# An encoder trunk in three-product float32: the DMA turn split into two steps, and another place for the seven-product units of w_down

## The chip, the cores and the metric

One core of a Trainium2 chip runs the whole program in one launch. The metric is the device time in microseconds (us), lower is better. Engine names are those of the profile: PE (TensorE matmul; its weight loads are PEld), DVE (VectorE), ACT (ScalarE), POOL (GpSimd), SP (SyncE, which here only issues DMAs). A small q behind a name (ACTq, SPq) is that engine's sequencer, which issues DMAs.

## The reference

Two layers over 256 tokens of width 2048, all float32. What matters here is the feed-forward half of each layer; the mixer ahead of it ends in a residual sum.

```python
def swiglu(h, w_gate_up, w_down):
    gate, up = jnp.split(h @ w_gate_up, 2, axis=-1)
    return (jax.nn.silu(gate) * up) @ w_down

for l in range(DEPTH):                       # DEPTH = 2, D_MODEL = 2048, D_FF = 5632
    ...                                      # token mixer, memory attention
    x = x + jnp.concatenate([tok_out, mem_out], axis=-1) @ w_out[l]
    x = x + swiglu(rms_norm(x, g_ffn[l]), w_gate_up[l], w_down[l])
```

## The kernel before

Every float32 product is made of three matmuls in a narrower type: a weight block is cast by ACT to `whi` (line 266), DVE subtracts to get the rest `wlo` (line 267), the activations are split in the same way, and `matmul3` (lines 199 to 201) issues hi x hi, hi x (the activation's rest) and (the weight's rest) x hi. All matmuls of the feed-forward half are 128x128 by 128x512.

The feed-forward half works in three chunks of the hidden width: gate/up columns 0 to 3, 4 to 7, and 8 to 10 (each 512 wide), and after each chunk the matching rows of `w_down`. A gate/up column and each half of `w_down` (called a and b here, 1024 output columns each) is one `Pair`: two blocks of 512 columns, both 128-token tiles. A `Pair` walks a list `order` of units; a unit is two 128-row blocks of the inner dimension against the two column blocks. Most units are computed with eight products (24 matmuls, method `eight`). Some, the quick ones, need seven (21 matmuls, method `seven`): DVE makes sums of weight blocks in place and in a tile `T` (lines 359 to 362), which is then cast and subtracted like a weight block. Sums of activations come from `activation_sums`. The quick units of a `Pair` also gather in four banks of their own (`m`); after the last of them, `inner` empties these into `e` tiles (lines 409 to 413) and, for `w_down`, adds them to the residual `x` (line 417). The other four banks (`acc`) are emptied by `outer` (line 425).

Between gate/up and `w_down` the gated activations must be transposed. `turned` does this with the DMA: ACT copies the tile into two planes of 16 bits (line 211), ACT's queue issues a transposing DMA (line 212), and ACT copies the result back into float32 order (line 215). ACT executes its instructions in order, so whatever stands behind line 215 waits for the landing. `turn_a` then splits the result for the matmuls. `add_residual` turns `x` in the same way at the end of a sub-layer.

The order of work is set by three things. The program counts steps: each half of a unit is one `tick`, and `later(n, f)` runs `f` n ticks on, so a turn is written between the units of the next `Pair`. The framework's scheduler then orders each engine's instructions: by the written order as a priority, but an instruction that is ready earlier by its own estimate may go ahead. And the buffers bound how far an engine runs ahead: three tiles for `whi` and for `wlo`, four for `raw` (the loaded weights), four `acc` and four `m` banks, 26 tiles for everything that `big` hands out.

The places of the quick units in `w_down` before: in half a third and fifth, in half b first and third (first and second chunk of a layer).

Of the kernel before, what the change touches and what calls it, by code (L numbers as in the profile page):

```python
# [12 lines left out]
U16 = mybir.dt.uint16  # L13
# [4 lines left out]
P = 128  # L18
# [36 lines left out]
def encoder(ctx: ExitStack, tc: tile.TileContext, x, mem, g_mix, g_ffn, w_in_a, g_v_a, w_spatial, b_spatial,  # L55
            w_in_b, g_q_b, g_k_b, g_mem, w_mem_kv, g_mq, g_mk, w_out, w_gate_up, w_down, rope_c, rope_s, out):
    nc = tc.nc
# [14 lines left out]
    def nm(s):  # L72
        uid[0] += 1
        return f"{s}_{uid[0]}"

    def big(dt=F32, shape=None):
        return room["p"].tile(shape or [P, NB], dt, tag="a", name=nm("a"))

    def small(n, long=False):
        return sp.tile([P, n], F32, tag=f"{'r' if long else 's'}{n}", name=nm(f"s{n}"), bufs=8 if long else 6)  # L80
# [4 lines left out]
    def v4(a):  # L85
        return a.rearrange("p (c n) -> p c n", n=P)
# [10 lines left out]
    def later(delay, fn):  # L97
        queue.append((clock[0] + delay, len(queue), fn))
# [22 lines left out]
    X = [[xp.tile([P, NB], F32, name=f"x_{t}_{j}") for j in range(4)] for t in range(NT)]  # L121
# [16 lines left out]
    def gslice(kind, l):  # L138
        return gcol[kind][:, 16 * l:16 * l + 16]
# [40 lines left out]
    def rsqrt_mean(ss, n, width, r=None):  # L180

        m = small(n)
        nc.gpsimd.tensor_scalar(m, ss, 1.0 / width, EPS, ALU.mult, ALU.add)
        if r is None:
            r = small(n, long=True)
        nc.gpsimd.tensor_tensor(r, m, mhalf[:, :n], ALU.pow)
        return r

    def split(src, shape):

        hi = big(F32R, shape)
        lo = big(F32R, shape)
        nc.scalar.copy(hi, src)
        nc.vector.tensor_tensor(lo, src, hi.bitcast(F32), ALU.subtract)  # L194
        return hi, lo
# [8 lines left out]
        for c in range(4):  # L204
            nc.tensor.transpose(dst[:, c * P:(c + 1) * P], src[:, c * P:(c + 1) * P], ident)  # L205

    def turned(src):

        a, b = big(F32, [P, 4, P]), big(F32, [P, 4, P])
        planes = a.bitcast(U16).rearrange("p c n -> p (c n)")  # L210
        nc.scalar.copy(planes.rearrange("p (h n) -> p h n", h=2), src.bitcast(U16).rearrange("p (n h) -> p h n", h=2))
        nc.scalar.dma_start_transpose(b.bitcast(U16).rearrange("p c n -> p (c n)").rearrange("p (c n) -> p c n", n=P),
                                      planes)
        whole = b.bitcast(U16).rearrange("p c n -> p (c n)").rearrange("p (h n) -> p n h", h=2)
        nc.scalar.copy(planes.rearrange("p (n h) -> p n h", h=2), whole)  # L215
        return a

    def square_sum(src, out):
        for i in range(2):
# [2 lines left out]
    def norm_piece(src, t, j, g, parts, keep):  # L222

        tp = misc()
        transpose4(src, tp)
        gained(tp, t, j, g, parts, keep)
        return tp
# [4 lines left out]
    def gained(tp, t, j, g, parts, keep):  # L232

        hi = keep(F32R, [P, 4, P])
        lo = keep(F32R, [P, 4, P])
        for c in range(4):
            gc = g[:, 4 * j + c:4 * j + c + 1]
            nc.scalar.activation(hi[:, c, :], v4(tp)[:, c, :], AF.Copy, scale=gc)
            nc.vector.scalar_tensor_tensor(lo[:, c, :], v4(tp)[:, c, :], gc, hi[:, c, :].bitcast(F32), ALU.mult,
                                           ALU.subtract)  # L240
            parts.put(4 * j + c, t, hi[:, c, :], lo[:, c, :])
        parts.whole[j, t] = hi, lo

    class Norm:
# [8 lines left out]
        def finish(self, out=(None, None)):  # L253
            self.r = []
            for t in range(NT):
                tot = small(1)
                nc.vector.tensor_reduce(tot, self.ss[t], AX.X, ALU.add)
                self.r.append(rsqrt_mean(tot, 1, D, out[t]))
# [53 lines left out]
    def activation_sums(a0, a1):  # L312

        q = big(F32, [P, 4, P])
        nc.vector.tensor_tensor(q[:, 0], a1[:, 0], a1[:, 1], ALU.subtract)
        nc.vector.tensor_tensor(q[:, 2], a1[:, 0], a0[:, 0], ALU.subtract)
        nc.vector.tensor_tensor(q[:, 1], a0[:, 0], q[:, 0], ALU.subtract)
        nc.vector.tensor_tensor(q[:, 3], a0[:, 1], q[:, 1], ALU.subtract)
        hi, lo = split(q, [P, 4, P])
        return [(hi[:, i, :], lo[:, i, :]) for i in range(4)]  # L320
# [277 lines left out]
    def add_residual(acc, j, norm, g, parts, dma):  # L598

        def turn(t):  # L600
            if dma:
                gained(turned(X[t][j]).rearrange("p c n -> p (c n)"), t, j, g, parts, kept)
            else:
                norm_piece(X[t][j], t, j, g, parts, kept)
            norm.add(X[t][j], t, j)
            if j == 3 and t == NT - 1:
                norm.finish()

        for t in range(NT):
            if acc:  # L610
                nc.vector.tensor_tensor(X[t][j], acc[t], X[t][j], ALU.add)
            later(1 + t, lambda t=t: turn(t))

    def residual_turns(j, norm, g, parts):
        add_residual(None, j, norm, g, parts, j < 2)
# [4 lines left out]
    for l in range(DEPTH):  # L620
# [105 lines left out]
        else:  # L726
# [12 lines left out]
            for c in range(3):  # L739
                acc = linear(hT, w, c * NB)  # L740
                attend(head_norm(acc, norm.r, ghead["q"], True), (5, 6, 10, 13), lambda: own["k"], lambda: own["v"],
                       lambda h, c=c: (4 * c + h) // 3, 4 * c, cat)
# [32 lines left out]
        for chunk in (range(0, 4), range(4, 8), range(8, 11)):  # L775
            aT, aS, half = Parts(), {}, {}
            quick = [2 * f + 1 for f in chunk[:2 if chunk[-1] < 10 else l]]

            def turn_a(a, t, f, aT=aT, aS=aS, half=half, quick=quick):
                whole = turned(a)  # L780
                i = 2 * f + 1
                if i in quick:
                    half[i, t] = big(F32, [P, 2, P])
                    nc.scalar.copy(half[i, t], whole[:, 2:4])
                    if t == NT - 1:
                        aS[i] = activation_sums(half[i, 0], half[i, 1])
                hi, lo = split(whole, [P, 4, P])
                for i in range(4):
                    aT.put(4 * f + i, t, hi[:, i, :], lo[:, i, :])

            pairs = {}
            for f in chunk:
                order, some = ((3, 4, 5, 0, 6, 1, 7, 2), 2) if f == 0 else ((0, 3, 1, 4, 2, 5, 6, 7), 3)
                pairs[f] = Pair(hF, sums, w_gate_up[l], f * NB, DFF + f * NB, order, fast[:some])
            for f, g in pairs.items():
                g.run(pairs.get(f + 1))
                for t in range(NT):
                    a = kp.tile([P, NB], F32, tag="sg", name=nm("sg"), bufs=2)
                    nc.scalar.activation(a, g.out[t][0], AF.Silu, scale=norm.r[t])
                    nc.vector.scalar_tensor_tensor(a, g.out[t][1], norm.r[t], a, ALU.mult, ALU.mult)  # L800
                    later(3 + t if f == chunk[-1] else 12 + t, lambda a=a, t=t, f=f: turn_a(a, t, f))
            last = chunk[-1] == 10
            every = [2 * f + c for f in chunk for c in range(2)]
            slow = [i for i in every if i not in quick]
            pairs = []
            for jj in range(2):
                order = list(slow)
                for n, i in enumerate(quick):
                    order.insert(2 * n + (0 if jj and not last else 2), i)
                into = [[X[t][2 * jj + n] for n in range(2)] for t in range(NT)]  # L810
                pairs.append(Pair(aT, aS, w_down[l], 2 * jj * NB, (2 * jj + 1) * NB, order, quick, into))
            for jj, g in enumerate(pairs):
                g.run(None if jj else pairs[1])
                for j in (2 * jj, 2 * jj + 1):
                    if last and l < DEPTH - 1:
                        residual_turns(j, next_norm, gslice("mix", l + 1), hT)
                    elif last:
                        for t in range(NT):
                            parts = 2 if j == 3 and t == NT - 1 else 1
                            for i in range(parts):  # L820
                                cs = slice(i * NB // parts, (i + 1) * NB // parts)
                                eng = nc.scalar if i else nc.sync
                                eng.dma_start(out[0, t * P:(t + 1) * P, j * NB + cs.start:j * NB + cs.stop],
                                              X[t][j][:, cs])
# [37 lines left out]
```

## Time and profile before

| | us |
|---|---|
| median of 3 runs | 2047.55 (2047.23 to 2048.38) |
| the profiled execution | 2049.83 |
| its span, first to last instruction | 2048.1 |
| PE busy | 2012.3 (98% of the span) |
| DVE busy | 1605.1 (78%) |
| ACT busy | 1214.8 (59%) |
| DMA queue of the weights (q1) | 56.2% of 16 engines' span |

PE is busy nearly always, so the time is the number of matmuls times their spacing, plus the places where PE stands still. Those are few and are found one by one in the order of time. A busy share says little on DVE and ACT here: they count only where PE waits for them.

### The profile page before, as it was taken

Reading aid. Unit: us, or ns where it says so; the run is one execution under the profiler, and the core shown is the slowest. Engines: PE = TensorE matmul, PEld = TensorE weight load, DVE = VectorE, ACT = ScalarE, POOL = GpSimd, SP = SyncE. Lnnn points to the kernel's source line nnn. Section 1 sums busy time; section 2 is a strip of 40 time slices with the busy share of each in tenths; the row PEclk is TensorE's granted clock in tenths of the full one; section 3 lists DMA queues with packets and bytes.
Section 4 is the critical chain, followed back from the end, with each engine's and each line's share of the span. In section 5 each row is a group of like instructions: output and inputs, shape, how many; then the busy total and the mean of one; then the engine's idle time right before and its main releaser. Section 6 shows DMA issues by size and latency. Waiting matters only on the chain.

```text
span 2048.1 us, 24306 instructions
## 1 busy us (share of the span) xinstructions
PE 2012.3 (98%) x9058; PEld 1655.7 (81%) x9058; DVE 1605.1 (78%) x1862; ACT 1214.8 (59%) x1509; POOL 50.5 (2%) x80
## 2 busy tenths in 40 slices
PE   8999999999999999999999999999999999999999
PEld 7888888878788887888888888877887888878877
DVE  5575558998889988797676876598888898878977
ACT  7765475666445664455766765666663476634653
POOL 2010000000000000000010000000000000000000
PEclk9999999999999999999999999999999999999999
DMA  9754585667556675567766445756665567655664
GB/s 330 248 176 161 188 217 175 205 199 224 199 187 219 197 225 198 180 225 223 211 224 204 158 133 162 209 174 212 221 220 181 185 221 218 218 175 196 192 209 144
DMA packets 265791, 411.79 MB, mean 201 GB/s; under 512 B 74428, under 2 KB 74792, under 8 KB 265672
## 3 DMA queue, kind: packets, MB, share of 16 engines
q1 hardware_dynamic: 198800, 385.79, 56.2%
q10 hardware_dynamic: 64824, 18.02, 5.0%
q0 software_dynamic: 2048, 6.42, 1.1%
q8 instruction: 71, 1.16, 0.2%
q14 instruction: 48, 0.39, 0.1%
HBM read 390.26 MB, written 4.19 MB: 193 GB/s over the span
## 4 chain that ended last, share of the span: by engine, by line
PE 88%; DVE 4%; ACT 3%; DMA 3%; issue 1%; SPq 0%; ACTq 0%; DVEq 0%
PE acc L201 26%; PE acc L200 25%; PE acc L199 25%; PE m L201 4%; PE m L199 4%; PE m L200 3%; DVE wlo L267 2%; ACT whi L266 2%; PE m L205 1%; DMA raw<-in_w_down 1%; DMA raw<-in_w_gate_up 1%; DMA a<-a 1%; PE m L512 0%; DVE x L417 0%; DVE x L425 0%
## 5 line engine op out<-in xcount | busy, mean ns | idle before, releaser
L267 DVE TENSOR_TENSOR wlo<-raw,whi 128x2048 fp32r<-128x2048 f32 (+2 forms) x465 | 837.5, 1822 | 223.3 <-ACT whi L266 219.6
L266 ACT CAST whi<-raw 128x2048 fp32r<-128x2048 f32 (+2 forms) x465 | 701.9, 1538 | 433.0 <-PE acc L200 377.7
L199 PE MATMUL acc<-whi,h 128*128 128x512 f32 x1440 | 562.9, 391 | 3.4 <-ACT whi L266 3.4
L200 PE MATMUL acc<-whi,h 128*128 128x512 f32 x1440 | 561.8, 390 | 0.0
L201 PE MATMUL acc<-wlo,h 128*128 128x512 f32 x1440 | 519.2, 391 | 2.8 <-DVE wlo L267 2.8
L199 PE MATMUL acc<-whi,a 128*128 128x512 f32 x1062 | 414.4, 392 | 10.5 <-DVE x L425 9.3
L200 PE MATMUL acc<-whi,a 128*128 128x512 f32 x1062 | 416.4, 392 | 0.0
L201 PE MATMUL acc<-wlo,a 128*128 128x512 f32 x1062 | 402.1, 392 | 0.2 <-DVE wlo L267 0.2
L201 PEld LDWEIGHTS acc<-wlo,h 128*128 128x128 f32 x1440 | 270.5, 188 | 62.1 <-DVE wlo L267 6.8
L199 PEld LDWEIGHTS acc<-whi,h 128*128 128x128 f32 x1440 | 270.6, 188 | 59.7 <-ACT whi L266 4.8
L200 PEld LDWEIGHTS acc<-whi,h 128*128 128x128 f32 x1440 | 270.5, 188 | 55.5
L199 PEld LDWEIGHTS acc<-whi,a 128*128 128x128 f32 x1062 | 200.1, 188 | 55.5 <-DVE x L425 13.1
L200 PEld LDWEIGHTS acc<-whi,a 128*128 128x128 f32 x1062 | 200.5, 189 | 42.0 <-DVE a L194 1.5
L201 PEld LDWEIGHTS acc<-wlo,a 128*128 128x128 f32 x1062 | 200.5, 189 | 41.8 <-DVE wlo L267 0.6
L266 ACT CAST whi<-T 128x1536 fp32r<-128x1536 f32 x82 | 121.4, 1480 | 129.8 <-PE acc L200 100.0
L267 DVE TENSOR_TENSOR wlo<-T,whi 128x1536 fp32r<-128x1536 f32 x82 | 143.5, 1750 | 17.8 <-ACT whi L266 17.7
L199 PE MATMUL m<-whi,a 128*128 128x512 f32 x264 | 104.1, 394 | 5.5 <-ACT whi L266 5.5
L215 ACT COPY a<-a 128x1024 uint16<-128x1024 uint16 x60 | 70.3, 1172 | 64.1 <-DMA a<-a 64.0
L200 PE MATMUL m<-whi,a 128*128 128x512 f32 x264 | 103.3, 391 | 0.0
L201 PE MATMUL m<-wlo,a 128*128 128x512 f32 x264 | 89.8, 393 | 2.1 <-DVE wlo L267 2.1
L359 DVE TENSOR_TENSOR raw<-raw 128x512 f32<-128x512 f32 x82 | 56.1, 684 | 41.6 <-DMA raw<-in_w_gate_up 37.9
L199 PEld LDWEIGHTS m<-whi,a 128*128 128x128 f32 x264 | 49.8, 189 | 18.9 <-ACT whi L266 8.8
(131 smaller groups left out, 1520.3 us busy)
## 6 DMA issues: line engine op xcount, KB each, us to landing
raw<-in_w_gate_up SPq DMA_DIRECT2D x352, 512.0 KB, 4.4
raw<-in_w_down SPq DMA_DIRECT2D x176, 512.0 KB, 5.0
raw<-in_w_out SPq DMA_DIRECT2D x32, 1024.0 KB, 5.2
raw<-in_w_in_a SPq DMA_DIRECT2D x24, 1024.0 KB, 5.1
raw<-in_w_in_b SPq DMA_DIRECT2D x24, 1024.0 KB, 5.1
raw<-in_w_mem_kv SPq DMA_DIRECT2D x16, 1024.0 KB, 5.1
raw<-in_w_in_a SPq DMA_DIRECT2D x7, 512.0 KB, 5.7
x<-in_x SPq DMA_DIRECT2D x8, 256.0 KB, 5.6
```

The source lines that it names most:

```text
L199: nc.tensor.matmul(out, lhsT=a[0], rhs=b[0], start=start, stop=False)
L200: nc.tensor.matmul(out, lhsT=a[1], rhs=b[0], start=False, stop=False)
L201: nc.tensor.matmul(out, lhsT=a[0], rhs=b[1], start=False, stop=stop)
L205: nc.tensor.transpose(dst[:, c * P:(c + 1) * P], src[:, c * P:(c + 1) * P], ident)
L215: nc.scalar.copy(planes.rearrange("p (n h) -> p n h", h=2), whole)
L266: nc.scalar.copy(hi[:, cut], raw[:, cut])
L267: nc.vector.tensor_tensor(lo[:, cut], raw[:, cut], hi[:, cut].bitcast(F32), ALU.subtract)
L359: nc.vector.tensor_tensor(raw[:, 0], raw[:, 0], raw[:, 1], ALU.add)
```

## The change

`turned` no longer returns a tile. It makes the first copy, issues the transposing DMA, and puts the copy back and all that follows into a function that runs two ticks later. `turn_a` is cut into `turn_a` and `split_a` for that, and `add_residual` hands over a function as well. And in the first two chunks of each layer half a of `w_down` now takes its quick units first and third, as half b did. The third chunk's halves keep theirs (third place). The instructions are the same in kind and number on each engine; only their order differs.

```diff
-    def turned(src):
+    def turned(src, ticks, then):
         a, b = big(F32, [P, 4, P]), big(F32, [P, 4, P])
 ...
-        nc.scalar.copy(planes.rearrange("p (n h) -> p h n", h=2), whole)
-        return a
+        def finish():
+            nc.scalar.copy(planes.rearrange("p (n h) -> p n h", h=2), back.rearrange("p (h n) -> p n h", h=2))
+            then(a)
+        later(ticks, finish)
 ...
-                gained(turned(X[t][j]).rearrange("p c n -> p (c n)"), t, j, g, parts, kept)
+                turned(X[t][j], 2, lambda a: gained(a.rearrange("p c n -> p (c n)"), t, j, g, parts, kept))
 ...
             def turn_a(a, t, f, aT=aT, aS=aS, half=half, quick=quick):
-                whole = turned(a)
+                turned(a, 2, lambda whole: split_a(whole, t, f, aT, aS, half, quick))
+            def split_a(whole, t, f, aT, aS, half, quick):
                 i = 2 * f + 1
 ...
-                    order.insert(2 * n + (0 if jj and not last else 2), i)
+                    order.insert(2 * n + (2 if last else 0), i)
```

What this moves is shown at three places of the first chunk of layer 0; the second chunk and layer 1 read alike. Line numbers of the changed kernel are 3 higher from line 211 on up to `add_residual`'s turn, and 5 higher behind it (211, 212, 215 become 212, 213, 216; 425 becomes 428).

First place, DVE from the last units of half a into half b. `raw_4344` is the block of half b's first unit (a quick one) and `T_4347` its sums, `raw_4423` that of its third (quick too), `whi_4387` the cast of `raw_4344`. The names `x` are the residual, `e` the emptied `m` banks. Before:

```order
L359 TENSOR_TENSOR raw_4423<-raw_4423 128x512
L267 TENSOR_TENSOR wlo_4388<-raw_4344,whi_4387 128x2048
L412 TENSOR_TENSOR e_4270<-m_4194,e_4270 128x512
L413 TENSOR_TENSOR e_4272<-m_4194,e_4271 128x512
L417 TENSOR_TENSOR x_1_90<-x_1_90,e_4271 128x512
L360 TENSOR_TENSOR T_4426<-raw_4423 128x512
L425 TENSOR_TENSOR x_0_89<-acc_4083,x_0_89 128x512
L417 TENSOR_TENSOR x_0_93<-x_0_93,e_4270 128x512
L417 TENSOR_TENSOR x_1_94<-x_1_94,e_4272 128x512
L425 TENSOR_TENSOR x_1_90<-acc_4090,x_1_90 128x512
```

And in the changed kernel, the same stretch:

```order
L420 TENSOR_TENSOR x_1_94<-x_1_94,e_4210 128x512
L363 TENSOR_TENSOR T_4347<-raw_4344 128x512
L270 TENSOR_TENSOR wlo_4353<-raw_4313,whi_4352 128x2048
L362 TENSOR_TENSOR raw_4423<-raw_4423 128x512
L364 TENSOR_TENSOR T_4347<-T_4347,raw_4344 128x512
L365 TENSOR_TENSOR T_4347<-T_4347,raw_4344 128x512
L363 TENSOR_TENSOR T_4426<-raw_4423 128x512
L270 TENSOR_TENSOR wlo_4388<-raw_4344,whi_4387 128x2048
L364 TENSOR_TENSOR T_4426<-T_4426,raw_4423 128x512
L365 TENSOR_TENSOR T_4426<-T_4426,raw_4423 128x512
L428 TENSOR_TENSOR x_0_89<-acc_4108,x_0_89 128x512
L428 TENSOR_TENSOR x_1_90<-acc_4112,x_1_90 128x512
```

The emptying of the `m` banks and its additions to `x` (lines 412 to 417) now end before the last block of half a is split (`wlo_4353`); the two rows that empty `acc` follow each other. PE's own order at this place is the same in both kernels, row for row.

Second place, ACT in the third gate/up pair, where the second pair's activations (`sg`) are turned. `whi_3562` and `whi_3593` in the later fence are casts of the weight blocks of the fourth and fifth unit. Before:

```order
L266 CAST whi_3529<-T_3488 128x1536
L211 COPY a_3662<-sg_3440 128x1024
L212 DMA_TRANSPOSE a_3663<-a_3662 128x8x128
L215 COPY a_3662<-a_3663 128x1024
L784 COPY a_3667<-a_3662 128x256
L193 CAST a_3669<-a_3662 128x512
L266 CAST whi_3562<-raw_3522 128x2048
L211 COPY a_3692<-sg_3443 128x1024
```

In the changed kernel:

```order
L269 CAST whi_3529<-T_3488 128x1536
L212 COPY a_3662<-sg_3440 128x1024
L213 DMA_TRANSPOSE a_3663<-a_3662 128x8x128
L212 COPY a_3685<-sg_3443 128x1024
L269 CAST whi_3562<-raw_3522 128x2048
L213 DMA_TRANSPOSE a_3686<-a_3685 128x8x128
L269 CAST whi_3593<-raw_3554 128x2048
L216 COPY a_3662<-a_3663 128x1024
L269 CAST whi_3597<-T_3557 128x1536
```

A copy and two casts of weights now stand between a transposing DMA and the copy that waits for it, and the second tile's DMA is issued before the first one's copy back.

Third place, ACT where the last gate/up pair of a chunk gives way to half a of `w_down`. Before, with eight-product units first:

```order
L211 COPY a_4135<-sg_4067 128x1024
L212 DMA_TRANSPOSE a_4136<-a_4135 128x8x128
L215 COPY a_4135<-a_4136 128x1024
L193 CAST a_4140<-a_4135 128x512
L211 COPY a_4156<-sg_4070 128x1024
L266 CAST whi_4172<-T_4114 128x1536
L212 DMA_TRANSPOSE a_4157<-a_4156 128x8x128
L266 CAST whi_4209<-raw_4165 128x2048
```

In the changed kernel, where `whi_4168` and `whi_4172` belong to the third unit (quick) and `whi_4219` to the fourth:

```order
L212 COPY a_4144<-sg_4067 128x1024
L269 CAST whi_4168<-raw_4120 128x2048
L269 CAST whi_4172<-T_4123 128x1536
L213 DMA_TRANSPOSE a_4145<-a_4144 128x8x128
L212 COPY a_4161<-sg_4070 128x1024
L216 COPY a_4144<-a_4145 128x1024
L213 DMA_TRANSPOSE a_4162<-a_4161 128x8x128
L193 CAST a_4186<-a_4144 128x512
L269 CAST whi_4219<-raw_4165 128x2048
```

Here only the second tile's copy stands between the first DMA and its copy back, while two casts have moved ahead of the DMA. In the turns of `x` at the end of a sub-layer the distance between a DMA and its copy back stays as it was.

More of the change, by code (lines that the diff above doesn't have):

```diff
@@ L205, in transpose4 @@
             nc.tensor.transpose(dst[:, c * P:(c + 1) * P], src[:, c * P:(c + 1) * P], ident)
-    def turned(src):
+    def turned(src, ticks, then):
         a, b = big(F32, [P, 4, P]), big(F32, [P, 4, P])
-        planes = a.bitcast(U16).rearrange("p c n -> p (c n)")
+        planes, back = [i.bitcast(U16).rearrange("p c n -> p (c n)") for i in (a, b)]
         nc.scalar.copy(planes.rearrange("p (h n) -> p h n", h=2), src.bitcast(U16).rearrange("p (n h) -> p h n", h=2))
[L212 to L215, printed above, removed]
-        return a
+        nc.scalar.dma_start_transpose(back.rearrange("p (c n) -> p c n", n=P), planes)
+        def finish():
+            nc.scalar.copy(planes.rearrange("p (n h) -> p n h", h=2), back.rearrange("p (h n) -> p n h", h=2))
+            then(a)
+        later(ticks, finish)
     def square_sum(src, out):
```

## The prediction

> **What bounds the kernel now.** I read the page first, then PE's waits, then windows around each place where PE stands still, then the timeline there. "Joint" below means the passage from one `Pair` to the next; a and b are the halves of `w_down`.
>
> ```profile
> PE 2012.3 (98%) x9058; PEld 1655.7 (81%) x9058; DVE 1605.1 (78%) x1862; ACT 1214.8 (59%) x1509; POOL 50.5 (2%) x80
> L215 ACT COPY a<-a 128x1024 uint16<-128x1024 uint16 x60 | 70.3, 1172 | 64.1 <-DMA a<-a 64.0
> ```
>
> PE is the bound. ACT stands 64.0 us behind transposing DMAs, but ACT is busy 59% only, so that figure is no saving by itself. What PE waits for (engine and line, what it waited for: us in total, times, longest):
>
> ```profile
> PE acc L199 <- DVE x L425: 9.3, 8, 2.3
> PE m L199 <- ACT whi L266: 6.7, 8, 1.3
> ```
>
> Eight waits for line 425 are two at each of four joints, a to b, in the first two chunks of both layers. Windows of PE alone (length, PE busy, number of matmuls, granted clock), three of them stretches that lose nothing, which hold the joints from one gate/up pair to the next (440), from gate/up to a (488) and from b to gate/up (570):
>
> ```profile
> 440.00:465.00 25.00, 25.00 (x112) 1.00 0.58 183
> 488.00:512.00 24.00, 24.00 (x107) 1.00 0.66 180
> 526.00:540.00 14.00, 9.72 (x39) 1.00 0.33 113
> 570.00:590.00 20.00, 20.00 (x90) 1.00 0.46 155
> 782.00:796.00 14.00, 10.18 (x41) 1.00 0.37 128
> 1536.00:1548.06 12.06, 7.72 (x30) 1.00 0.47 159
> 1548.06:1551.48 3.42, 3.42 (x9) 0.50 0.00 0
> 1790.00:1800.65 10.65, 8.09 (x35) 1.00 0.65 218
> 1800.65:1810.89 10.24, 8.73 (x19) 0.50 0.12 45
> 418.00:428.00 10.00, 7.86 (x34) 1.00 0.67 205
> 1429.00:1439.00 10.00, 7.91 (x34) 1.00 0.65 200
> 1990.00:2000.00 10.00, 8.60 (x37) 1.00 0.34 84
> ```
>
> 24.00 us with 107 matmuls is 0.224 us each, 4.46 per us. By that rate the four joints a to b miss 23.4, 21.4, 30.0 and 39.1 matmuls: 5.2 + 4.8 + 6.7 + 8.8 = 25.5 us. The stretches at 418 and 1429 (the third gate/up pair of each layer) miss 10.6 each, 2.4 us each; that at 1990 misses 7.6, 1.7 us. Together 32.0 of the 2048 us: more than that the change cannot touch.
>
> One joint a to b in the order of time (PE; then DVE; then ACT):
>
> ```profile
> 527.73 0.39 PE L199 MATMUL m<-whi,a 128*128 128x512 f32 x1
> 530.77 0.50 PE L199 MATMUL acc<-whi,a 128*128 128x512 f32 x1 [1.52 <-DVE x L425]
> 532.57 0.50 PE L199 MATMUL acc<-whi,a 128*128 128x512 f32 x1 [0.84 <-DVE x L425]
> 534.87 0.50 PE L199 MATMUL m<-whi,a 128*128 128x512 f32 x1 [1.33 <-ACT whi L266]
> 536.66 0.73 PE L201 MATMUL m<-wlo,a 128*128 128x512 f32 x2 [0.60 <-DVE wlo L267]
> 524.83 0.69 DVE L359 TENSOR_TENSOR raw<-raw 128x512 f32<-128x512 f32 x1 [0.18 <-DMA raw<-in_w_down]
> 525.43 2.28 DVE L267 TENSOR_TENSOR wlo<-raw,whi 128x2048 fp32r<-128x2048 f32 x1
> 527.64 0.68 DVE L412 TENSOR_TENSOR e<-m,e 128x512 f32<-128x512 f32 x1
> 528.24 0.68 DVE L413 TENSOR_TENSOR e<-m,e 128x512 f32<-128x512 f32 x1
> 530.04 0.68 DVE L425 TENSOR_TENSOR x<-acc,x 128x512 f32<-128x512 f32 x1
> 531.84 0.68 DVE L425 TENSOR_TENSOR x<-acc,x 128x512 f32<-128x512 f32 x1
> 521.85 1.92 ACT L266 CAST whi<-raw 128x2048 fp32r<-128x2048 f32 x1 [3.99 <-PE acc L200]
> 533.34 1.47 ACT L266 CAST whi<-T 128x1536 fp32r<-128x1536 f32 x1 [9.57 <-PE acc L200]
> ```
>
> Four holes. The first two are DVE's: between its split at 525.43 and the first line 425 at 530.04 stand four small operations, two of them emptying the `m` banks of half a's last quick unit. The last two are not: the cast of `T` at 533.34 had waited 9.57 us for a free `whi` tile, since PE still holds the tiles of half a's last two units, and PE then waits out the cast (1.47) and the subtraction.
>
> **The change, part by part.**
>
> *Quick units first and third in half a.* The `m` banks are then emptied two units earlier. In DVE's new order the rows of lines 412 to 417 stand ahead of half a's last split, and at the joint the two rows of line 425 follow each other. Would they be in time? DVE's last big split ahead of them needs the cast at 521.85, which PE lets go 5.9 us before its first matmul of half b (527.73). Counted from that cast's start: the cast 1.92, the split 2.28 and two sums of 0.6 (the distance of 527.64 and 528.24) make 5.4; the first line 425 ends at 6.1, the second at 6.7. PE asks for the first bank six matmuls into half b, at 7.2, for the second at 7.9. So both holes close with about 1.2 us to spare. Worth: 9.3 us of idle, plus 0.17 at each of eight restarts (a matmul counts as busy for 0.39 or more while starts come 0.224 apart): 10.7, and I take 11.0 with the small wait ahead of the fourth joint. The other two holes stay: `T`'s cast and subtraction have the same predecessors as before, and PE's order there is unchanged. Bounds: 5.5 (half of it) to 13.
>
> *The half clock.* The rows at 1548 and 1800 run at clock 0.50: 9 matmuls in 3.42 us instead of 15.2 (1.4 us), and 19 in 8.73 busy us instead of 38.9 (4.5 us, of which about 0.5 are the restarts counted above): 5.4 us. Both follow a joint at once; the joints at 526 and 782, hardly shorter, show none. What remains of a joint is two holes (1.33 and 0.60) within 2.5 us, so the chance falls but does not vanish; I take half, 2.7, with 0 to 5.4 as ends.
>
> The Trainium skill, "TensorE: Matmul & The Clock Gate", section "HAM oscillation — how this bites in real kernels", puts the abstract rule as no PE-idle gaps over about 3.4 us. The trace disagrees: its longest idle gap ahead of either half-clock stretch is 2.3 us (the row of waits for line 425), and the clock fell all the same. By the rule alone the remaining holes would cost no clock and the sum would be 2.7 us lower.
>
> *The turn in two steps.* The stall at 421 is an ACT chain:
>
> ```profile
> 413.00 1.25 ACTq L212 DMA_TRANSPOSE a<-a  x1
> 417.35 1.18 ACT L215 COPY a<-a 128x1024 uint16<-128x1024 uint16 x1 [4.39 <-DMA a<-a]
> 419.39 1.89 ACT L266 CAST whi<-raw 128x2048 fp32r<-128x2048 f32 x1
> 421.34 0.50 PE L199 MATMUL acc<-whi,h 128*128 128x512 f32 x1 [1.49 <-ACT whi L266]
> ```
>
> The cast at 419.39 could have started at 413 but for line 215. In the new order a copy (1.04) and two casts (1.9 each) stand between the DMA and line 215, 4.8 us against a landing of 4.3, and the cast PE asks for is the first of them. Both stretches (418 and 1429) go: 2 x 2.4 = 4.8 us; bounds 3 to 5.5. The turns of `x` keep two ACT rows between DMA and copy back in both orders: nothing. The stall at 1990 (third chunk of layer 1) stays within 0.5 either way: the cast of `T` there still stands behind the first copy back. The number of transposes, of their issues (1.25 us of ACT's queue each) and of weight loads stays; SP loads the same blocks in another row order, and one weight load moves ahead of two output writes in the last half; POOL has nothing moved.
>
> *What it may cost: the joint from gate/up to a.* It loses nothing today (24.00 of 24.00), so there is no gain to be had, and it now starts with a quick unit, while the new order has a double wait for DMAs in it. Today's rows there, and the landings of all 60 transposes:
>
> ```profile
> 490.57 1.91 ACT L266 CAST whi<-raw 128x2048 fp32r<-128x2048 f32 x1 [1.70 <-PE acc L200]
> 493.40 1.05 ACT L211 COPY a<-sg 128x1024 uint16<-128x1024 uint16 x1 [0.30 <-DVE sg L800]
> 494.48 1.25 ACTq L212 DMA_TRANSPOSE a<-a  x1
> 498.60 1.17 ACT L215 COPY a<-a 128x1024 uint16<-128x1024 uint16 x1 [4.15 <-DMA a<-a]
> 499.80 0.62 ACT L193 CAST a<-a 128x512 fp32r<-128x512 f32 x1
> DMA to landing us min/median/max: 3.1/4.9/9.7
> L267 DVE TENSOR_TENSOR wlo<-T,whi 128x1536 fp32r<-128x1536 f32 x82 | 143.5, 1750 | 17.8 <-ACT whi L266 17.7
> ```
>
> Count from the end of the last gate/up pair, E. PE has a quick, an eight-product and a quick unit to do (21 + 24 + 21 matmuls, 14.8 us) before it asks for the fourth unit's cast. ACT: the gated tile is there at about E + 4 (today 2.9: the cast at 490.57 starts when PE lets go of the last gate/up unit, and line 211 starts at 493.40; the new order adds a subtraction for `T`, 1.75 by the group below, ahead of the gating, and takes some sums away); line 211's copy 1.05, landing 4.1 as here, copy back 1.17, the second issue 1.25, a small cast 0.62, the cast 1.91: E + 14.1. So 0.7 us to spare; at the shortest landing (3.1) 1.7; at the median (4.9) 0.1 late; at the longest (9.7) 4.9 late. Over four joints 0 to 19.6 us; I take 0.8 in all, by the row at this very place. DVE has 28.6 us of work over the six units around the joint (six rows of 2.28, two of 1.75, eighteen small ones of about 0.63) against PE's 30.9 (138 matmuls), so it keeps up, and the sums for the first unit stand ahead of the joint in its order.
>
> The sum against the profiled execution: 2049.83 - 11.0 - 2.7 - 4.8 + 0.8 = 2032.1, that is 17.7 less. The profiled execution lies 2.3 above the median, so the median comes to 2047.55 - 17.7 = 2029.8 us.
>
> **The rivals.**
>
> *A, the new joint leaks.* Landings of 6 to 7 us instead of 4.1, because two transposes now follow closely and share the queues with the loads of a quick unit: 2 to 3 us late at four joints, 10 us given back: about 2040. For: the longest landing is 9.7. Against: they go one after the other, the second only after the first has landed.
>
> *B, only one half of the change works.* DVE's line 425 still comes late at a to b, since ahead of it in DVE's queue stand sums of a block whose load lands late (the 0.18 at 524.83 was such a wait): 11.0 and the clock's 2.7 stay, 4.8 go: about 2043. Against: that load can now be issued some 4 us earlier, when DVE has done the split that frees its buffer.
>
> *C, the clock never falls.* With 4.3 us of idle time a joint cut to 1.9, no half-clock stretch is left: 2.7 more, about 2027. For: two of four joints, with more idle time, had none. The page named above would have it so.
>
> *D, slower: the stall moves to gate/up to a.* That joint takes over what a to b has today. `outer` of the gate pair, the gating and the sums for the first quick unit meet on DVE as they met at 526; if the sums are not made when the gate pair ends, PE waits for them and for `T`'s cast, 25.5 us over four joints, and a to b gains only the 11.0 and 2.7, the turn 4.8: 7.0 slower, about 2055. It decides when DVE ends the sums later than about 2 us after the gate pair. Against: in DVE's new order they stand before the last subtraction of that pair's `m` banks, and the joints at 440 and 570 lead into a quick unit too, the second out of a half with the new places, and lose nothing.
>
> **How the numbers follow.** Forecast 0.56 (own range 2024 to 2035), C 0.11, A 0.17, B 0.10, D 0.06. From no change a measurement here can tell about 0.2%, 4 us, so faster means below 2043.5, slower above 2051.6. Forecast, C and nearly all of A count as faster, half of B: 0.87; the rest of B and a bad A as no change: 0.07; D: 0.06. The range goes from C with the upper ends of the other terms (13 and 5.5 instead of 11 and 4.8, no new cost: 2047.55 - 13 - 5.4 - 5.5 = 2023.7, less 1.7 for the hole at 1990) to A at its worst: 2022 to 2041.
>
> **What the profile after would show.** PE's eight waits for line 428 (once 425) gone or below 2 us in all; the waits for the cast of `T` (about 1.3) and for `wlo` (0.6) at the four joints still there; ACT's wait for transposes well below 64 us; no hole in the third gate/up pair of each layer; at gate/up to a no hole over 1 us; the half clock at two joints or fewer. The forecast is wrong if a hole of 2 us or more opens ahead of half a's fourth unit, or if the first rows of line 428 at a to b start more than 2 us after PE's last matmul of that bank.

## The result, and the profile after

The changed kernel takes 2029.45 us (median of four runs, 2027.68 to 2030.63) against 2047.91 for the kernel before: ratio 0.9909, 95% interval 0.9897 to 0.9922. Its profiled execution took 2030.63 us, with a span of 2028.8 (before: 2048.1). In the second comparison, on another chip, the ratio was 0.9912 (0.9898 to 0.9926).

The page's line of busy times, then waits (engine and line, what it waited for: us in total, times, longest), of the changed kernel:

```profile
PE 2006.1 (99%) x9058; PEld 1656.6 (82%) x9058; DVE 1603.5 (79%) x1862; ACT 1213.8 (60%) x1509; POOL 50.5 (2%) x80
PE m L199 <- ACT whi L269: 5.7, 6, 1.3
PE m L201 <- DVE wlo L270: 2.4, 4, 0.6
PE acc L199 <- DVE x L428: 1.4, 3, 0.6
ACT a L216 <- DMA a<-a: 37.1, 21, 3.6
```

DVE and ACT are as busy as before. PE's eight waits for line 425 (9.3 us) have become three for line 428 (1.4); the four for the cast of `T` (1.33 each) and the four for `wlo` (0.60) are still there. ACT stands 37.1 us behind transposes instead of 64.0. Windows of PE (length, PE busy, matmuls, granted clock, DMA share, GB/s): the third gate/up pair, the four joints a to b, one half-clock stretch, and two joints from gate/up to a:

```profile
418.00:428.00 10.00, 10.00 (x45) 1.00 0.94 320
524.00:538.00 14.00, 11.88 (x49) 1.00 0.34 123
779.00:793.00 14.00, 11.44 (x47) 1.00 0.33 116
1526.00:1540.00 14.00, 12.07 (x44) 0.88 0.36 126
1782.00:1796.00 14.00, 11.49 (x42) 0.88 0.36 122
1534.48:1537.89 3.41, 3.32 (x8) 0.50 0.00 0
500.00:512.00 12.00, 11.32 (x49) 1.00 0.68 212
1503.00:1513.00 10.00, 9.24 (x40) 1.00 0.61 177
```

The pair at 418 has lost its hole (45 matmuls, it had 34). The joints miss half to three quarters of what they missed. The clock still falls twice. And the joint from gate/up to a, which lost nothing, now misses 4 or 5 matmuls. The first joint a to b (PE, then DVE, then ACT):

```profile
527.77 0.50 PE L199 MATMUL acc<-whi,a 128*128 128x512 f32 x1 [0.19 <-DVE x L428]
530.77 0.50 PE L199 MATMUL m<-whi,a 128*128 128x512 f32 x1 [1.33 <-ACT whi L269]
532.56 0.73 PE L201 MATMUL m<-wlo,a 128*128 128x512 f32 x2 [0.60 <-DVE wlo L270]
527.02 1.29 DVE L428 TENSOR_TENSOR x<-acc,x 128x512 f32<-128x512 f32 x2
529.24 1.47 ACT L269 CAST whi<-T 128x1536 fp32r<-128x1536 f32 x1 [7.14 <-PE acc L200]
```

To compare fourteen profiles I add up, over PE, how far the starts of successive matmuls lie apart beyond the undisturbed spacing (0.226 us for 512 columns, 0.113 for 256, 0.109 for 128). I call that the lost time; it takes in idle time, restarts and half clock. The matmuls are the same in all fourteen, and their undisturbed spacings add up to 1981.4 us; the lost time is by its definition all the rest of the distance from the first matmul to the last:

| lost time, us | in all | halves a and joints a to b | gate/up to a | third gate/up pair | at 1990 | half-clock stretches, length |
|---|---|---|---|---|---|---|
| before | 56.9 | 27.2 | 0 | 5.6 | 2.0 | 13.7 |
| changed | 37.8 | 16.0 | 4.4 | 0.1 | 0 | 6.8 |
| turn alone | 51.0 | 32.4 | 0 | 0.1 | 0.5 | 20.5 |
| places alone | 68.7 | 34.1 | 4.3 | 7.7 | 1.9 | 34.1 |
| two steps in the last pair only | 44.8 | 12.2 | 4.5 | 5.5 | 0 | 3.4 |
| two steps in all but the last pair | 41.9 | 15.1 | 7.6 | 0.1 | 1.8 | 10.2 |
| copy back into the gated tile | 22.7 | 0 | 4.7 | 0.1 | 0 | 0 |
| the same, 25 buffers | 38.7 | 12.9 | 8.5 | 0.1 | 0 | 3.4 |
| the same (26), old places | 20.8 | 2.6 | 0 | 0.1 | 0 | 0 |

The last column is no loss of its own: half of it is contained in the columns ahead. From before to changed the lost time falls by 19.1, the span by 19.3: joints 11.2, third pair 5.5, the hole at 1990 2.0, small holes all over the span 4.8 together (the largest at 926, 1.4, and between 1350 and 1380, about 1), less 4.4 for the new holes at gate/up to a.

### The profile page after: what moved, and what is told of

Same layout as the page of the kernel before. It is cut to its first block, busy times and chain, and to the rows that moved or that the text cites. A ratio compares the mean times of both kernels' runs of the same rounds, so it can differ in the third digit from the quotient of the medians.

```text
span 2028.8 us, 24312 instructions
## 1 busy us (share of the span) xinstructions
PE 2006.1 (99%) x9058; PEld 1656.6 (82%) x9058; DVE 1603.5 (79%) x1862; ACT 1213.8 (60%) x1509; POOL 50.5 (2%) x80
## 4 chain that ended last, share of the span: by engine, by line
PE 92%; DVE 3%; DMA 3%; ACT 1%; issue 1%; SPq 0%; DVEq 0%; ACTq 0%
PE acc L201 26%; PE acc L200 26%; PE acc L199 26%; PE m L201 4%; PE m L199 4%; PE m L200 4%; DMA a<-a 2%; DVE wlo L270 2%; ACT whi L269 1%; PE m L205 1%; PE m L515 0%; DMA x<-in_x 0%; PE m L661 0%; DVE T L365 0%; DMA raw<-in_w_in_a 0%
## 5 line engine op out<-in xcount | busy, mean ns | idle before, releaser
L201 PEld LDWEIGHTS acc<-wlo,h 128*128 128x128 f32 x1440 | 270.6, 188 | 56.9 <-DVE wlo L270 1.4
L216 ACT COPY a<-a 128x1024 uint16<-128x1024 uint16 x60 | 70.2, 1170 | 37.3 <-DMA a<-a 37.1
```

The source lines that it names most:

```text
L201: nc.tensor.matmul(out, lhsT=a[0], rhs=b[1], start=False, stop=stop)
L216: nc.scalar.copy(planes.rearrange("p (n h) -> p n h", h=2), back.rearrange("p (h n) -> p n h", h=2))
```

## The experiments

All were timed beside the kernel before, and the ratios are to that kernel.

**The turn alone, the places alone.** In the first, the line of the places is that of before; in the second, `turned` is.

```diff
 turn alone:
-                    order.insert(2 * n + (2 if last else 0), i)
+                    order.insert(2 * n + (0 if jj and not last else 2), i)
 places alone (against the kernel before):
-                    order.insert(2 * n + (0 if jj and not last else 2), i)
+                    order.insert(2 * n + (2 if last else 0), i)
```

> The turn in two steps alone; half a's quick units stay second and fourth. Theory (the two halves act at different places and add up): the holes of the third gate/up pair (2.8 and 2.7 us before, 0.1 after) and the hole of the third chunk at 1990 (2.0) go, the joints a to b stay at 27.6 us of lost time as before, and gate/up to a loses nothing, since it starts with an eight-product unit again: 2047.9 - 7.5 = 2040.4, with the small scattered holes (3.6) up to 2036.8; range 2036 to 2043. Rival (the order of w_down does it all, since it gives ACT and DVE their slack everywhere): 2046 to 2048. In either case the first transposes at gate/up to a should land in 3 to 4.2 us as before if it is the new places that make them late, in 6.5 to 7 us if the two steps do.

> Half a's quick units first and third alone; the turn stays in one step. Theory: the joints a to b lose 16 us instead of 27.6 as in the changed kernel, the third gate/up pairs keep their 2.8 and 2.7, and gate/up to a loses 4 us or more, since the first unit asks for its cast while ACT waits for a landing: 2047.9 - 11.3 + 4.4 = 2041, range 2037 to 2046. Rival (the new cost at gate/up to a comes from the two steps): that joint loses under 1 us, and the time is 2036 to 2038. A second rival: the copy back now stands ahead of the casts of three quick units and the joint opens by 2 to 4 us at each of four places: 2046 to 2053.

Turn alone: 2041.42 us, 0.9952 (0.9938 to 0.9966). The time is the first theory's; the joints, which it left at 27.6 us, lost 32.4 in the profile. Places alone: 2061.04 us, 1.0052 (1.0038 to 1.0066), slower than before, and slower than all three forecasts: the second rival, which comes nearest, ends at 2053, 1.0025 of the kernel before. So the halves don't add up: 9.8 us faster, 9.8 slower, and together 18.

At the joints neither half does much by itself. Taken without the half clock, the joints lose 20.4 us before, 22.2 with the turn alone, 18.7 with the places alone and 12.6 with both. (Half of the stretches is taken off: 6.8, 10.2, 15.4 and 3.4; the places alone have one more stretch, at 1439, outside the joints.) The clock has a large part in the rest. An estimate of its cost is (1 - granted clock) x time, over all timed executions: 12.3 us for the kernel before beside these two, 7.8 for the turn alone, 16.1 for the places alone, 3.0 and 3.2 for the changed kernel in its two comparisons. Added up, the two halves alone would save 0.7 us of that; together they save 9, about half of the 18.

What is late differs. Places alone, ACT and then DVE ahead of the first joint:

```profile
498.80 1.25 ACTq L212 DMA_TRANSPOSE a<-a  x1
512.32 1.25 ACTq L212 DMA_TRANSPOSE a<-a  x1
513.69 1.92 ACT L266 CAST whi<-raw 128x2048 fp32r<-128x2048 f32 x1 [1.40 <-PE acc L201]
520.45 1.18 ACT L215 COPY a<-a 128x1024 uint16<-128x1024 uint16 x1 [4.83 <-DMA a<-a]
522.18 3.72 ACT L266 CAST whi<-raw 128x2048 fp32r<-128x2048 f32 x2
524.12 2.29 DVE L267 TENSOR_TENSOR wlo<-raw,whi 128x2048 fp32r<-128x2048 f32 x1 [2.46 <-ACT whi L266]
```

The second transpose of the chunk's last pair stands 13.5 us behind the first in ACT's queue and lands 8.1 us after its issue. ACT stands in front of its copy back, with the casts of half a's last unit and half b's first behind it, and DVE's whole queue slips. Turn alone, DVE waits too, but for a load:

```profile
515.02 0.69 DVE L362 TENSOR_TENSOR raw<-raw 128x512 f32<-128x512 f32 x1 [4.42 <-DMA raw<-in_w_down]
527.64 2.29 DVE L270 TENSOR_TENSOR wlo<-raw,whi 128x2048 fp32r<-128x2048 f32 x1
531.65 1.28 DVE L428 TENSOR_TENSOR x<-acc,x 128x512 f32<-128x512 f32 x2
```

The landings at gate/up to a settle where the new cost there comes from: with the turn alone the first transposes land in 5.9, 3.1, 3.1 and 3.7 us and at most 0.4 us is lost; in the changed kernel in 7.0, 6.6, 7.1 and 6.5. It is the quick unit put first, and not the two steps.

**Two steps in the last pair only, or in all but the last.** To see which turns the joints need:

```diff
-                turned(a, 2, lambda whole: ...)
+                turned(a, 2 if f == chunk[-1] else 0, lambda whole: ...)     # last pair only
+                turned(a, 0 if f == chunk[-1] else 2, lambda whole: ...)     # all but the last
-        later(ticks, finish)
+        later(ticks, finish) if ticks else finish()                         # both, and `one step` below
```

> New places; of the ffn's turns only the two of a chunk's last gate/up pair are made in two steps, the others in one. Theory (the places alone came out slower because ACT stood 4.8 to 6.0 us in front of the copy back of a chunk's last turn, ahead of two casts that DVE and PE then had late): the joints a to b lose 16 to 18 us again instead of 34.5, and only the stalls of the third gate/up pair (5.5) and the small ones around other turns (about 4) stay: 9 slower than the changed kernel, that is 0.995 of the kernel before (0.993 to 0.997). Rival (the places need the two steps in the inner turns, which give ACT its slack for the whole chunk): the joints stay at 30 or more, 1.002 to 1.006.

> The counterpart: new places, two steps for all turns but those of a chunk's last gate/up pair. Theory: the joints a to b lose 30 us or more as with the places alone, gate/up to a about 4, and the third gate/up pair nothing: 9 to 10 faster than the places alone, that is 1.000 of the kernel before (0.998 to 1.003). Rival (as above, the inner turns make the difference): 0.990 to 0.993.

> The changed kernel itself, on the chip of the next three runs, as their yardstick: 0.990 to 0.992 of the kernel before.

The yardstick came to 2031.20 us, 0.9912 (0.9898 to 0.9926). Last pair only: 2037.56 us, 0.9945 (0.9929 to 0.996), the theory's number. All but the last: 2032.48 us, 0.9917 (0.9901 to 0.9933), the rival's number, so the theory falls as I had put it. Either half of the two steps closes the same holes. ACT in the second kernel shows why one step in the last pair is harmless there:

```profile
493.16 1.28 ACTq L213 DMA_TRANSPOSE a<-a  x1
500.10 1.17 ACT L216 COPY a<-a 128x1024 uint16<-128x1024 uint16 x1 [4.36 <-DMA a<-a]
502.90 1.25 ACTq L213 DMA_TRANSPOSE a<-a  x1
504.58 3.71 ACT L269 CAST whi<-raw 128x2048 fp32r<-128x2048 f32 x2
508.66 1.18 ACT L216 COPY a<-a 128x1024 uint16<-128x1024 uint16 x1
```

The second transpose is issued 9.7 us behind the first instead of 13.5, in a place where three casts cover it, and no wait stands ahead of the late casts. I read this so: it is not the one step that hurts at the joint but where the order that the scheduler writes then leaves the second transpose, and that order changes with turns far from the joint.

A rival to this remains. Both kernels keep the turns of `x` in two steps, which the places alone do not. The kernel with one step and the spare buffer (below) speaks against it: its turns of `x` are in two steps too, and it issues the second transpose of a chunk's last pair 12 to 16 us behind the first all the same. New places with two steps for `x` alone were not run. The table shows where each group of turns earns its own: the third pair's 5.5 us hang on the inner turns, the hole at 1990 on the last pair's.

**Copying back into the gated tile.** The second step of a turn writes into the gated tile (`sg`), which is free by then, and not into the tile of planes. A split then needs one buffer of the ffn's pool less.

```diff
-    def turned(src, ticks, then):
+    def turned(src, ticks, then, own=False):
 ...
-            nc.scalar.copy(planes.rearrange("p (n h) -> p n h", h=2), back.rearrange("p (h n) -> p n h", h=2))
-            then(a)
+            to, flat = (src.rearrange("p (c n) -> p c n", n=P), src.bitcast(U16)) if own else (a, planes)
+            nc.scalar.copy(flat.rearrange("p (n h) -> p n h", h=2), back.rearrange("p (h n) -> p n h", h=2))
+            then(to)
 ...
-                turned(a, 2, lambda whole: split_a(whole, t, f, aT, aS, half, quick))
+                turned(a, 2, lambda whole: split_a(whole, t, f, aT, aS, half, quick), True)
```

> The changed kernel, but in the ffn the second step copies back into the gated tile itself and not into the tile of planes, so that a split needs one buffer fewer (26 of 26 at the last split of a chunk, where it was 27). PE's order at the joints a to b then has no matmuls of half a left behind the first unit of half b. Theory (the two holes that stay at each joint, 1.33 and 0.60 us of idle time, come from weight tiles that half a's last units hold because one split is late for want of a buffer): the joints lose 1 us each or less instead of 3.2 to 5.0, no half clock: 2029.5 - 12 to 13 = 2017, range 2015 to 2021. Rival (the cast of the sums of weights is late there by its own chain, whatever PE's order): the holes stay, 2028 to 2031. Against both: the gated tile is held longer, and with two of them the next gating waits: up to 2034.

2017.79 us, 0.9835 (0.982 to 0.9849), and 2016.56 us, 0.9832 (0.9817 to 0.9847), the second time: the theory's figure, 15 to 16 us less than the changed kernel by the ratios. All four joints lose nothing, and no half clock is left ahead of PE's last matmul:

```profile
523.00:537.00 14.00, 14.00 (x64) 1.00 0.47 156
```

In the kernel before and in the changed one PE's order leaves 22 matmuls of half a's last two units behind half b's first unit. The first of them wants the second half (`lo`, line 194) of the chunk's last split, which DVE writes only when half b's first unit is under way. The changed kernel at the first joint (half b starts at 526.06):

```profile
532.42 0.69 DVE L194 TENSOR_TENSOR a<-a,a 128x512 fp32r<-128x512 f32 x1
533.16 0.50 PE L200 MATMUL acc<-whi,a 128*128 128x512 f32 x1
```

At the four joints that row starts 6.1 to 6.8 us after half b's first matmul. In this kernel it starts 18.1 to 19.1 us ahead of it, and the 22 stand ahead of half b. That is 22 x 0.226 = 5.0 us of work for PE while DVE empties the banks, and the weight tiles of half a's last two units are free in time for the cast of `T`. The control takes the buffer away again:

```diff
-FFN_TILES = 26
+FFN_TILES = 25
```

> The kernel that copies back into the gated tile (2017.8 us, 0.9835), with 25 buffers in the ffn's pool instead of 26; nothing else. Theory (it was the one buffer that closed the joints): PE's order there is the changed kernel's again, with matmuls of half a behind half b's first unit, and the time is the changed kernel's: 0.990 to 0.992. Rival (the gain came from the other tile that is written, or from buffers that come free earlier in general): 0.983 to 0.987.

2032.12 us, 0.9925 (0.9911 to 0.994). The theory had 0.990 to 0.992, the rival 0.983 to 0.987; the interval reaches the changed kernel's 0.9912 and stays far from the rival. The 22 matmuls are left behind as before, and PE's waits at the joints are the old ones to the hundredth (1.33 and 0.60 at each):

```profile
PE m L199 <- ACT whi L270: 5.7, 6, 1.3
PE m L201 <- DVE wlo L271: 2.4, 4, 0.6
```

So it is the one buffer.

**With the buffer there, are the two halves of the change still worth anything?** The kernel above, once with half a's quick units third and fifth again (the recorded expectations call these places second and fourth), once with the ffn's turns in one step.

```diff
 old places:
-                    order.insert(2 * n + (2 if last else 0), i)
+                    order.insert(2 * n + (0 if jj and not last else 2), i)
 one step:
-                turned(a, 2, lambda whole: split_a(whole, t, f, aT, aS, half, quick), True)
+                turned(a, 0, lambda whole: split_a(whole, t, f, aT, aS, half, quick), True)
```

> The kernel that copies back into the gated tile, once more, as the yardstick of the next three on their chip: 0.982 to 0.985 of the kernel before.

> The yardstick with half a's quick units second and fourth again, as in the kernel before. Theory (the spare buffer closes the joints a to b by itself, whatever the places, since nothing of half a is left behind half b's first unit; and the joint gate/up to a loses nothing with an eight-product unit first): 3 to 4.5 us less than the yardstick, 0.980 to 0.983. Rival (the sums of half a's last quick unit still come late on DVE, 1.7 us at four joints and a stretch of half clock behind some): 7 to 15 us more, 0.987 to 0.991.

> The yardstick with the ffn's turns in one step (new places, copy back into the gated tile). Theory (a spare buffer does not help where ACT stands in front of a landing): the stalls of the third gate/up pair return (5.5) and some small ones (2 to 4), and the second transpose of a chunk's last pair may again be issued late: 8 to 20 us more than the yardstick, 0.987 to 0.994. Rival (one step was slow only because buffers were short): within 2 us of the yardstick.

Old places: 2012.21 us, 0.9811 (0.9796 to 0.9825), the fastest kernel here and 4.3 us below its yardstick's median: the theory's range. Windows of PE from gate/up into half a and at two joints a to b, and DVE ahead of the first of these, nearly row for row as with the turn alone:

```profile
480.00:515.00 35.00, 35.00 (x154) 1.00 0.64 190
523.00:537.00 14.00, 14.00 (x64) 1.00 0.70 223
777.00:791.00 14.00, 14.00 (x63) 1.00 0.49 158
514.59 0.69 DVE L363 TENSOR_TENSOR raw<-raw 128x512 f32<-128x512 f32 x1 [3.94 <-DMA raw<-in_w_down]
527.20 2.28 DVE L271 TENSOR_TENSOR wlo<-raw,whi 128x2048 fp32r<-128x2048 f32 x1
533.48 1.87 DVE L429 TENSOR_TENSOR x<-acc,x 128x512 f32<-128x512 f32 x3
```

DVE waits 3.94 us for the same load and empties the banks later than with the turn alone (533.48 against 531.65), and PE loses 1.45 us inside half a, at 517, and nothing at the joint. The new places repaired a joint that the missing buffer had broken; with the buffer they only cost their 4 us at gate/up to a. Beside the turn alone (0.9952) the one buffer is worth 29 us, beside the changed kernel 15.

One step: 2048.60 us, 0.9993 (0.9981 to 1.0006), 32 us above its yardstick, where I had expected 8 to 20. With the same places but without the buffer the two steps, those of `x` with them, are worth 29 us (1.0052 for the places alone against 0.9909), so the buffer does little to their worth; what raises it from 9.8 us is the new places. One step with the buffer and the old places was not run. The lost time is 51.9 against 24.9; 19.1 of it lies in the third gate/up pairs, where ACT stands up to 9.24 us in front of one landing, and 10.2 us run at half clock:

```profile
ACT sg L217 <- DMA a<-a: 86.2, 26, 9.2
434.85 1.16 ACT L217 COPY sg<-a 128x1024 uint16<-128x1024 uint16 x1 [9.24 <-DMA a<-a]
```

**Finishing the last turns four steps later.** In the changed kernel, and with the spare buffer:

```diff
-                turned(a, 2, lambda whole: ...)
+                turned(a, 4 if f == chunk[-1] else 2, lambda whole: ...)
```

> The changed kernel, but the last turns of a chunk finish four steps later instead of two. ACT then casts the fourth unit's weights ahead of the first part of the split (0.62 us) and behind the copy back. Theory (the 4.4 us lost at gate/up to a are ACT's: landing, copy back, cast in that order): the fourth unit is asked for 0.6 us earlier at four joints, 1.5 to 2.4 us less: 2027.0 to 2028.0. Rival (the split then comes later than before and PE waits for its products instead): 2030 to 2034. Rival (PE's own order hides it): 2029 to 2030.

> The same with the last turns of a chunk finished four steps later. Theory (with the joints a to b closed, the 4.4 us at gate/up to a are the largest loss left, and ACT's order there gives back 1.9 of them, as in the kernel with four steps alone): 1 to 2.5 us less than its yardstick, 0.981 to 0.984. Rival (the later split meets a joint that has no slack left): 1 to 3 us more.

2031.87 us, 0.9905 (0.9889 to 0.9921), and with the buffer 2013.91 us, 0.9821 (0.9807 to 0.9836). By the times neither can be told from its yardstick (0.9909 or 0.9912, and 0.9832). In the profiles the lost time at gate/up to a falls from 4.4 to 2.5 and from 4.2 to 2.6, as expected of ACT's order: cast ahead of the split's first part, 0.62 us at a time. The rest hangs on the landing, and that was not taken away by itself.

## Why the prediction was right, and where it was not

The time (2029.8 forecast, 2029.45 measured) came out, but that it came so close is luck. By the profiles the four terms of the sum are worth 12.3 us (7.8 + 3.4 + 5.5 - 4.4) where 17.7 were forecast, and two that were put at nothing, the hole at 1990 and the small holes, add 6.8.

*Quick units first and third: 11.0 for the holes, 2.7 for the clock.* In the profiles the joints gained 11.2, of it 3.4 from the clock and 7.8 from the holes. The failed step is "Would they be in time?", which found 1.2 us to spare. It let DVE's last split ahead of line 428 start when its cast ends. ACT and DVE in the changed kernel:

```profile
520.18 1.92 ACT L269 CAST whi<-raw 128x2048 fp32r<-128x2048 f32 x1 [3.57 <-PE acc L200]
523.01 0.70 DVE L363 TENSOR_TENSOR T<-raw 128x512 f32<-128x512 f32 x1
523.61 2.30 DVE L270 TENSOR_TENSOR wlo<-raw,whi 128x2048 fp32r<-128x2048 f32 x1
```

The cast starts 5.9 us ahead of half b's first matmul (526.06), as counted, and ends at 522.10. The split starts 1.5 us later, since DVE has four sums of half b's quick units ahead of it, from 521.21 on; they stand there in the order that the section on the change lists. At the other joints the split is 1.3 to 2.0 us behind the cast's end. So the first line 428 starts at 527.02, 6.8 us after the cast's start and not 5.4, and PE still waits 0.2 to 0.6 at three of the four joints. The prediction's own rows have the same lag: 525.43 for the split, 523.77 for the cast's end.

And the gain does not belong to this part of the change alone: with the places alone the same cast starts at 522.18 behind a landing, and the joints lose as much as before or more (34.1 in the table against 27.2). The prediction costed each half at its own place and added; the runs show 9.8 lost, 9.8 gained, 18 gained together.

*The two holes that stay* were forecast to the hundredth, but explained by half: "PE still holds the tiles of half a's last two units" is right, and the experiment with the buffer shows what made it hold them.

*The half clock.* Half of it was to stay; in the two profiles half did (6.8 of 13.7 us). Over all timed executions more went: by the same estimate as above 9.1 us in the kernel before and 3.2 in the changed one, both from the second comparison, so 6 us against the 2.7 of the sum. The Trainium skill, "TensorE: Matmul & The Clock Gate", section "HAM oscillation — how this bites in real kernels", would have had the clock stay up with gaps under about 3.4 us. The changed kernel disagrees as the one before did: its longest hole at a joint is 1.33 us, and two stretches of 3.41 us follow. Rival C is out for this profile; of the nine timed executions of the changed kernel one (2028.37 us) has a granted clock of 1.000.

*The turn in two steps: 4.8.* 5.5 measured at that place, in the changed kernel and with the turn alone.

*The hole at 1990: "within 0.5 either way".* It went, 2.0 us. The step looked at the cast of `T`, which does stand behind the first copy back in both orders; but the hole hangs on the next cast. ACT there before, and in the changed kernel:

```profile
1988.25 1.48 ACT L266 CAST whi<-T 128x1536 fp32r<-128x1536 f32 x1
1991.99 0.59 ACT L409 COPY e<-m 128x512 f32<-128x512 f32 x1 [1.32 <-PE m L200]
1992.47 1.91 ACT L266 CAST whi<-raw 128x2048 fp32r<-128x2048 f32 x1
```
```profile
1970.32 1.48 ACT L269 CAST whi<-T 128x1536 fp32r<-128x1536 f32 x1 [0.18 <-ACT a L216]
1973.30 1.91 ACT L269 CAST whi<-raw 128x2048 fp32r<-128x2048 f32 x1
1975.62 0.58 ACT L412 COPY e<-m 128x512 f32<-128x512 f32 x1
```

Before, the cast was queued behind a copy that waits for PE's own `m` bank; now it goes ahead of it. The kernel with two steps in all but the last pair has the old order and the old hole (1.8). The small holes (4.8) were not in the sum at all.

*Gate/up to a: 0.8.* It cost 4.4. By its own row the sum had 0.7 us to spare there, so the 0.8 was an allowance. The step that failed took the landing "by the row at this very place", 4.1 us. ACT and PE in the changed kernel:

```profile
492.43 1.28 ACTq L213 DMA_TRANSPOSE a<-a  x1
499.42 1.17 ACT L216 COPY a<-a 128x1024 uint16<-128x1024 uint16 x1 [3.47 <-DMA a<-a]
499.42 1.25 ACTq L213 DMA_TRANSPOSE a<-a  x1
501.24 1.90 ACT L269 CAST whi<-raw 128x2048 fp32r<-128x2048 f32 x1
503.20 0.50 PE L199 MATMUL acc<-whi,a 128*128 128x512 f32 x1 [0.46 <-ACT whi L269]
```

The landing took 7.0, 2.9 more than counted. The chain ran late by less, since the second issue (1.25), which I had put in series, starts together with the copy back. Rival A had the landings (6 to 7 us; measured 6.5 to 7.1), and for their cause the loads of a quick unit, which is likely but not shown; it had 2 to 3 us a joint where 0.8 to 1.4 were lost. No hole over 1 us opened, as forecast. Rival B did not come about. Its picture, line 428 late behind sums in DVE's queue, is what the changed kernel still shows in small and the turn alone, with its wait of 4.42 us for a load, in full. Rival D did not either: gate/up to a lost 4.4 us, not 25.5.

## What to carry to other kernels

When an in-order queue carries both work for the bound engine and waits for transfers, put the wait two steps of work behind the issue: here that was worth 10 us with the old places, 29 with the new, and 32 with the new and the spare buffer. Before repairing a stall at a joint by shifting the order of work, ask why the bound engine had nothing left to do there: one buffer too few had put 22 matmuls behind the joint, and giving it back was worth 15 us here, 29 with the old places, and made half of the change superfluous. Two edits that touch the same queues have no price each; cost them together, from the order that both produce.

## What the runs showed of the hardware

A transpose of 256 KB between buffers of the chip lands 3.0 to 3.1 us after its issue at best, in 4.8 to 5.7 in the median of a kernel, and in 8.4 to 10.7 at worst. The first one at gate/up to a sorts by the two loads of weights (512 KB each) issued nearest to it. Where they are issued some 4 us ahead (the kernel before, and old places in two steps: 12 transposes) it lands in 3.1 to 4.1, but for two of 5.8 and 5.9. Where they come 0.4 to 1.9 ahead (8 transposes) it lands in 4.9 to 6.1, and where they follow within 0.6 (492.59 behind 492.43; 32 transposes) in 6.5 to 7.3. The four of the kernel with one step and the spare buffer (5.4 to 7.7) do not sort so. That the loads slow it is the likeliest reading; it was not measured alone.

Half clock comes in stretches of 3.41 us and multiples. At the same pattern of holes, 1.33 and 0.60 us within 2.5 us, it followed 8 of 24 joints in six profiles (the changed kernel in both comparisons, four steps later, two steps in the last pair only, in all but it, 25 buffers). In the four profiles with the spare buffer and two steps it never came; their holes lie far apart, and behind the first 20 us the longest is 1.45 us. The length of one hole does not decide it: in the kernel with one step and the spare buffer a hole of 3.58 us, ending at 1448.86, is followed by a clock of 1.00. A stretch of 3.41 us costs about 1.7, an estimate: half of it.
